# A hybrid decoder block on one core: low halves of the projection weights kept in DRAM after the first token group, and pick indices laid out in pairs

## The chip, the cores and the metric

One core of one Trainium2 chip runs the whole block for one sequence of 1024 tokens. The metric is the device time of one execution in microseconds (us), the median of several executions. Engines are named as the profile names them: PE (TensorE matmul), PEld (its weight loads), DVE (VectorE), ACT (ScalarE), POOL (GpSimd) and SP (SyncE, which here only issues DMAs).

## What is computed

The reference is a decoder block in fp32 with width 1024. Cut to what matters here:

```python
h = rms_norm(x, norm1_g) * (1 + sc1) + sh1          # adaLN: mod = silu(c) @ w_ada + b_ada
b, c, hc, q, k, v = split(h @ w_in)                 # 2304 columns
mixed = concat(short_conv(b, c, hc), window_attention(q, k, v))
x = x + g1 * (mixed @ w_out)                        # 1024 columns
h2 = rms_norm(x, norm2_g) * (1 + sc2) + sh2
# PEER: 8 heads, two key tables of 128, top 16 of each, top 16 of the 256 sums
q = h2 @ wq                                         # 2048 columns
sa, sb = q_a @ keys_a, q_b @ keys_b
eidx, top = top16(top16(sa) + top16(sb))            # an expert = one row of u and of v
x = x + g2 * sum_k softmax(top)_k * gelu(u[eidx_k] . h2) * v[eidx_k]
```

## The kernel before, in words

**Two phases.** The front computes everything up to the choice of the experts, for three groups of tokens in turn (`GROUPS`: 384, 384 and 256 tokens). The dense phase then runs PEER for the first 640 tokens as two large matrix products over all 16384 experts (L816 with the table `uT`, L873 with `v`), while a background task gathers the chosen rows for the last 384 tokens (L741, L760, L768).

**Precision.** Each fp32 factor is split into a high part, rounded to fp32r, and the low rest; a product is high times high, high times low and low times high. For a weight, ACT rounds it (`wH`, L268) and POOL subtracts (`wL`, L269).

**Projections.** `proj` (L260 to L274) makes 128 output columns of `w_in`, `w_out` or `wq` for one group. It goes in two half chunks of 512 rows: SP fetches 256 KB of weights (`wraw`, L265), ACT makes `wH`, POOL makes `wL`, and PE runs 12 matmuls (L272). Each of the three tiles has three buffers. A group calls it 18 + 8 + 16 = 42 times, so each group has 84 half chunks and the front has 252. Every group fetches and splits the same weights again.

**Order of the work.** The front is written in program order and a scheduler lays out each engine's queue; on the chip every queue runs in order. `bg` lets background tasks advance. Into the first group these are the adaLN products (`ada`) and the bias table. Into the second and third group it is the previous group's `finish_topk`, which runs `select` and then `spread` or `place` for each block of 128 tokens.

**`select`** (L593 to L671) runs per block. It copies the indices of the key picks to bf16 (`idf`, L595), forms 64 candidate sums per head (`cand`, L598), takes the top 16 of them (`top16`), decodes their positions, and picks the two indices by one-hot tiles (`hot1`): compare with `rank` (L660), multiply by the indices (L662), add up in halves (L666, L668). The index operand of L662 has the stride 0 in its innermost dimension.

**`spread`** (five blocks in all) turns each token's picks into one-hot tiles `oi` (in the pattern ACT, POOL, DVE, DVE over the tokens, L703 to L706) and `oj` (DVE, L711), multiplies them on PE (L714), copies the result to `stage` (ACT, L715) and writes `stage` to DRAM (`gd`, SP, L717).

**SP's queue** holds the weight fetches (L265), the `x` chunks (L306), the row stores (L519), the stores of `h2` (L533), the `stage` stores (L717), the adaLN fetches (L157) and at the end of the front the first loads of the dense phase (L796, L827, L937).

Of the kernel before, what the change touches and what calls it, by code (L numbers as in the profile page):

```python
# [10 lines left out]
F32 = mybir.dt.float32  # L11
F32R = mybir.dt.float32r
BF16 = mybir.dt.bfloat16
# [3 lines left out]
ALU = mybir.AluOpType  # L17
# [4 lines left out]
P = 128  # L22
# [4 lines left out]
PH = 8  # L27
# [15 lines left out]
NCAND = CSTART[-1]  # L43
# [31 lines left out]
def hymba_peer_kernel(ctx: ExitStack, tc: tile.TileContext, a, out: bass.AP):  # L75
    nc = tc.nc
    V, A, G, PE = nc.vector, nc.scalar, nc.gpsimd, nc.tensor

    const = ctx.enter_context(tc.tile_pool(name="const", bufs=1))
    dram = ctx.enter_context(tc.tile_pool(name="dram", bufs=1, space=DRAM))  # L80
# [23 lines left out]
    def col(name, i=0):  # L104
        return cols[:, COLS[name][0] + i:COLS[name][0] + i + 1]
# [7 lines left out]
    h2s = dram.tile([2, P, NC, DT], F32, name="h2s")  # L113
    gd = dram.tile([DT // TB, P, P, TB], F32, name="gd")
    biasd = dram.tile([P, NH, 384], F32, name="biasd")

    cond = const.tile([P, 8], F32, name="cond")
    A.activation(cond, colr("c"), AF.Silu)
# [8 lines left out]
    wp = fe.enter_context(tc.tile_pool(name="wp", bufs=3))  # L127
    hot = ExitStack()
    lv = hot.enter_context(tc.tile_pool(name="lv", bufs=1, side="right"))
    sel = hot.enter_context(tc.tile_pool(name="sel", bufs=1, side="right"))  # L130
# [96 lines left out]
    def bg(us):  # L227
        for t in list(tasks):
            t[2] += us * t[1]
            while t[2] >= 1.0:  # L230
                t[2] -= 1.0
                with tc.high_priority(offset=-BACK):
                    end = next(t[0], 0) == 0
                if end:
                    tasks.remove(t)
                    break
# [12 lines left out]
    def bigt(pool, name, dt, cnt=2):  # L249
        return [pool.tile([P, 4, TM], dt, name=f"{name}{i}", tag="big") for i in range(cnt)]  # L250

    def tmp(name, w=TM, **k):
        if name == "q":
            k["bufs"] = QB
        return tp.tile([P, w], F32, name=name, **k)

    def ch(t, c):
        return t[c // 4][:, c % 4, :]

    def proj(wsrc, sH, sL, T):  # L260
        bg(24 * T / 2400 + 0.5)
        pt = pj.tile([P, TM], F32, name="pj")
        for h in range(2):
            w = wp.tile([P, 4, P], F32, name="wraw")
            nc.sync.dma_start(w, wsrc[:, 4 * h:4 * h + 4, :])  # L265
            wH = wp.tile([P, 4, P], F32R, name="wH")
            wL = wp.tile([P, 4, P], F32R, name="wL")
            A.copy(wH, w)  # L268
            G.tensor_tensor(wL, w, wH.bitcast(F32), op=ALU.subtract)  # L269
            for c in range(4):  # L270
                for k, (wl, sr) in enumerate(((wH, sH), (wH, sL), (wL, sH))):
                    PE.matmul(pt[:, 0:T], wl[:, c, :], sr[h][:, c, 0:T],  # L272
                              start=(h == 0 and c == 0 and k == 0), stop=(h == 1 and c == 3 and k == 2))
        return pt[:, 0:T]  # L274
# [29 lines left out]
    def xchunk(c, t0, T):  # L304
        x = tmp("x", bufs=XB)[:, 0:T]
        nc.sync.dma_start(x, a["xT"][:, c, t0:t0 + T])  # L306
        return x
# [24 lines left out]
    def front(t0, T, hs, nxt):  # L332
        nb = T // P
        nd = max(0, min(nb, (DT - t0) // P))
        hH, hL = hs
        kH = t1.tile([P, P + TM], F32R, name="kH")
        kL = t1.tile([P, P + TM], F32R, name="kL")
        if t0:
            A.copy(kH[:, 0:P], kpH.bitcast(F32))
            A.copy(kL[:, 0:P], kpL.bitcast(F32))  # L340
        kc = tmp("k", bufs=1)[:, 0:T]
        A.copy(kc, proj(a["w_in"][4], hH, hL, T))
        qT = [tmp("y", bufs=4)[:, 0:T] for c in range(4)]
        for c in range(4):
            A.copy(qT[c], proj(a["w_in"][c], hH, hL, T))
        vT = tmp("q")
        A.copy(vT[:, 0:T], proj(a["w_in"][5], hH, hL, T))

        def conv():
            ys = []  # L350
            for cc in range(4):
                cs = tmp("q")[:, 0:T]
                A.copy(cs, proj(a["w_in"][6 + 3 * cc], hH, hL, T))
                yield
                u = tp.tile([P, TM + 2], F32, name="u", bufs=1)
                V.tensor_copy(u[:, 0:2], upv[:, cc, :])
                V.tensor_tensor(u[:, 2:T + 2], cs, proj(a["w_in"][7 + 3 * cc], hH, hL, T), op=ALU.mult)
                yield
                V.tensor_copy(upv[:, cc, :], u[:, T:T + 2])
                y = tmp("y", bufs=4)[:, 0:T]  # L360
                A.activation(y, u[:, 0:T], AF.Copy, scale=col("cw", cc))
                V.scalar_tensor_tensor(y, u[:, 1:T + 1], col("cw", 4 + cc), y, op0=ALU.mult, op1=ALU.add)
                V.scalar_tensor_tensor(y, u[:, 2:T + 2], col("cw", 8 + cc), y, op0=ALU.mult, op1=ALU.add)
                V.tensor_tensor(y, y, proj(a["w_in"][8 + 3 * cc], hH, hL, T), op=ALU.mult)
                ys.append(y)
                yield
            bc = group_stats(ys, T)
            if CY:
                yield
            for cc, y in enumerate(ys):  # L370
                V.scalar_tensor_tensor(y, y, col("cg", cc), bc(cc), op0=ALU.mult, op1=ALU.mult)
                A.copy(mc[0][:, cc, 0:T], y)
                G.tensor_tensor(mc[1][:, cc, 0:T], y, mc[0][:, cc, 0:T].bitcast(F32), op=ALU.subtract)
# [110 lines left out]
        mH, mL = (mc[0], ma[0]), (mc[1], ma[1])  # L484
# [3 lines left out]
            rn = norm_stats(lambda c: xchunk(c, *nxt), nxt[1]) if nxt else None  # L488
        x2T = bigt(ba, "x2T", F32)
        for c in range(NC):  # L490
            pt = proj(a["w_out"][c], mH, mL, T)
            V.scalar_tensor_tensor(ch(x2T, c)[:, 0:T], pt, mod[:, 16 + c:17 + c], xchunk(c, t0, T),
                                   op0=ALU.mult, op1=ALU.add)
        h2 = bigt(bb, "h2H", F32R), bigt(bb, "h2L", F32R)
        h2H, h2L = h2
# [45 lines left out]
        iu = [lv.tile([P, 2 * PH, 16], U32, name="iu", bufs=5) for b in range(nb)]  # L541
# [14 lines left out]
        for mm in range(0, 16, 2):  # L556
            qs = []
            for m in (mm, mm + 1):
                qq = tmp("q")[:, 0:T]
                A.copy(qq, proj(a["wq"][m], h2H, h2L, T))  # L560
                qs.append(qq)
                if held and m % 2 == KLAG:
                    keys(*held)
                    held = None
            held = (mm, mm + 1), qs
# [25 lines left out]
            V.max_index(u[:, 8:16], v[:, 8:16], s)  # L591

    def select(va, iu):  # L593
        idf = sel.tile([P, 2 * PH, 16], BF16, name="idf")
        A.copy(idf, iu)  # L595
        va4 = va.rearrange("p (h s) k -> p h s k", s=2)
        id4 = idf.rearrange("p (h s) k -> p h s k", s=2)
        cand = sel.tile([P, PH, NCAND], F32, name="cand")  # L598

        def pairs(a0, na, nbb, st):  # L600
            o4 = cand[:, :, st:st + na * nbb].rearrange("p h (x y) -> p h x y", y=nbb)
# [24 lines left out]
        def ft(name, **k):  # L626
            return sel.tile([P, n], F32, name=name, **k)
# [29 lines left out]
        for s, src in ((0, aab), (1, stb)):  # L657
            r = ft(f"pick{s}", tag=("a3", "st3")[s])
            hot1 = sel.tile([P, PH, 16, 16], BF16, name="hot1")
            V.tensor_tensor(hot1, src.rearrange("p (h k) -> p h k", h=PH).unsqueeze(2).to_broadcast([P, PH, 16, 16]),  # L660
                            rank.unsqueeze(1).to_broadcast([P, PH, 16, 16]), op=ALU.is_equal)
            V.tensor_tensor(hot1, hot1, id4[:, :, s, :].unsqueeze(3).to_broadcast([P, PH, 16, 16]), op=ALU.mult)  # L662
            yield
            m = 8
            while m > 1:
                V.tensor_tensor(hot1[:, :, 0:m, :], hot1[:, :, 0:m, :], hot1[:, :, m:2 * m, :], op=ALU.add)  # L666
                m //= 2
            V.tensor_tensor(r.rearrange("p (h k) -> p h k", h=PH), hot1[:, :, 0, :], hot1[:, :, 1, :], op=ALU.add)  # L668
            yield
            res.append(r)  # L670
# [349 lines left out]
    with tc.tile_pool(name="ada", bufs=2, side="right") as ap:  # L1020
        T0 = GROUPS[0][1]
        wt = gat.tile([P, 4, D], F32, name="wt", tag="stage")
        slots = [wt[:, c, :] for c in range(4)]
        x0 = bigt(bb, "x0", F32)
        wide = [t.rearrange("p c t -> p (c t)")[:, 0:D] for t in bigt(ba, "wringa", F32) + bigt(bb, "wringb", F32)]
        first = ada_start(ap, slots[0:3] + wide, slots[3])
        next(first)
        for h in range(2):
            nc.sync.dma_start(x0[h][:, :, 0:T0], a["xT"][:, 4 * h:4 * h + 4, 0:T0])

        def x0c(c):
            return ch(x0, c)[:, 0:T0]

        for _ in range(3):
            next(first)
        r0 = norm_stats(x0c, T0)
        for c in range(NC):
            G.tensor_tensor(x0c(c), x0c(c), r0[:, 0:T0], op=ALU.mult)
        for _ in first:
            pass  # L1040
        hs = norm1(*GROUPS[0], x0c)
        table.append(add(bias_table(ap), 1.0))
        rest.append(add(ada((2, 4, 3, 5), ap, slots), ADA_RATE, ADA0))
        hs, prev = front(*GROUPS[0], hs, nxts[0])
        for t in rest:
            drain(t)
    gbc = tc.tile_pool(name="gb", bufs=1, side="right")
# [82 lines left out]
```

## Time and profile before

| | us |
|---|---|
| median of three executions | 2853.47 |
| lowest and highest | 2850.66 and 2859.0 |
| the profiled execution, its own time | 2857.49 |
| its span in the profile | 2855.7 |

The span is 1.8 us shorter than the profiled execution's own time. Busy times are sums over an engine's instructions; PE and PEld overlap each other, and a PE busy time counts pipelined matmuls to their modelled ends. A wait row names who waited, for whom, for how long in sum, how often, and the longest.

### The profile page before, as it was taken

The page shows a single profiled execution, that of the slowest core. Times are in us where ns is not written, and L with a number is a line of the kernel's source. Part 1 is how long each engine was busy: PE and PEld are TensorE (multiplying, and loading weights), DVE is VectorE, ACT ScalarE, POOL GpSimd, SP SyncE. Part 2 cuts the span into 40 slices and gives each one's busy share as a digit, 9 for nine tenths or more (in the row PEclk, how much of TensorE's full clock was granted, in tenths as well). Part 3 has the DMA queues.
Part 4 walks back from the last instruction along what each step waited for, and adds up shares of the span by engine and source line. Part 5 has one row for each costly group of instructions (what it writes and reads, how often), then busy time and mean ns, then how long its engine had stood idle before and what let it go on. Part 6 is the DMA issues. An engine that isn't in the chain of part 4 may idle for free.

```text
span 2855.7 us, 45148 instructions
## 1 busy us (share of the span) xinstructions
PE 2700.5 (95%) x15679; PEld 2445.9 (86%) x15679; DVE 2373.4 (83%) x4845; ACT 1093.9 (38%) x2193; POOL 1721.7 (60%) x1491
## 2 busy tenths in 40 slices
PE   8899988999787889999999999999999999999998
PEld 6788978789786778889989989999989889988987
DVE  3665898877899697888988888888889888888887
ACT  2455468775586643222322222232222222222221
POOL 3444475656667744666666666666666666666661
PEclk7999999999999989999999999999999999999999
DMA  7647423464344677999999999999999999999995
GB/s 243 217 155 232 121 103 115 158 216 156 97 151 137 234 227 229 342 337 343 326 322 346 340 344 335 349 325 332 347 334 324 325 339 346 333 336 345 324 327 193
DMA packets 345157, 764.31 MB, mean 268 GB/s; under 512 B 31296, under 2 KB 130016, under 8 KB 341984
## 3 DMA queue, kind: packets, MB, share of 16 engines
q0 software_dynamic: 112320, 408.99, 39.6%
q1 hardware_dynamic: 231168, 349.81, 37.4%
q8 instruction: 123, 2.02, 0.3%
q10 hardware_dynamic: 1440, 2.62, 0.2%
q14 instruction: 106, 0.87, 0.1%
HBM read 702.06 MB, written 59.24 MB: 267 GB/s over the span
## 4 chain that ended last, share of the span: by engine, by line
PE 44%; DMA 8%; DVE 6%; issue 5%; POOL 2%; ACT 1%; SPq 0%; DVEq 0%; POOLq 0%; ACTq 0%
PE pv L873 22%; PE pa L816 21%; DMA vraw<-in_v 4%; DMA uraw<-in_uT 2%; DVE pq L768 2%; DVE vdL L860 1%; POOL rows L741 1%; ACT vdH L859 1%; DVE rows L760 1%; DMA wraw<-in_wq 1%; DMA rows<-in_v,eidx 1%; POOL uL L800 1%; DVE dacc L892 0%; DVE gw L835 0%; PE pj L272 0%
## 5 line engine op out<-in xcount | busy, mean ns | idle before, releaser
L816 PE MATMUL pa<-h,uH 128*128 128x320 f32 x4096 | 772.9, 311 | 15.2 <-ACT uH L799 6.2
L816 PEld LDWEIGHTS pa<-h,uH 128*128 128x128 f32 x4096 | 648.8, 189 | 23.1 <-ACT uH L799 7.2
L873 PE MATMUL pv<-vdH,wdH 128*128 128x512 f32 x1275 | 500.0, 392 | 18.0 <-DVE dacc L892 16.4
L269 POOL TENSOR_TENSOR wL<-wraw,wH 128x512 fp32r<-128x512 f32 x252 | 351.5, 1402 | 272.7 <-ACT wH L268 249.4
L873 PE MATMUL pv<-vdL,wdH 128*128 128x512 f32 x1275 | 497.8, 390 | 0.1
L873 PE MATMUL pv<-vdH,wdL 128*128 128x512 f32 x1275 | 496.8, 390 | 0.0
L816 PE MATMUL pa<-h,uL 128*128 128x320 f32 x2048 | 469.2, 310 | 2.3 <-POOL uL L800 2.3
L800 POOL TENSOR_TENSOR uL<-uraw,uH 128x512 fp32r<-128x512 f32 x256 | 342.4, 1338 | 163.3 <-ACT uH L799 142.7
L741 POOL DMA_INDIRECT rows<-in_u,eidx x257 | 260.8, 1015 | 157.1 <-DVE aw L760 83.2
L741 POOL DMA_INDIRECT rows<-in_v,eidx x254 | 253.7, 999 | 164.6 <-DVE pq L768 117.1
L816 PEld LDWEIGHTS pa<-h,uL 128*128 128x128 f32 x2048 | 344.6, 189 | 3.3 <-POOL uL L800 3.3
L768 DVE SCALAR_TENSOR_TENSOR pq<-rows,aw,pq 128x1024 f32<-128x1024 f32 x253 | 324.5, 1282 | 3.3 <-DMA rows<-in_v,eidx 0.8
L892 DVE TENSOR_TENSOR dacc<-dacc,pv 128x512 f32<-128x512 f32 x310 | 211.9, 684 | 134.0 <-PE pv L873 111.4
L859 ACT CAST vdH<-vraw 128x512 fp32r<-128x512 f32 x255 | 153.5, 619 | 439.0 <-DMA vraw<-in_v 366.4
L799 ACT CAST uH<-uraw 128x512 fp32r<-128x512 f32 x256 | 158.3, 619 | 418.9 <-DMA uraw<-in_uT 340.5
L760 DVE CUSTOM_DVE_ANT_0 rows<-rows,pq 128x1024 f32<-128x1024 f32 x257 | 307.5, 1212 | 12.5 <-DMA rows<-in_u,eidx 10.9
L873 PEld LDWEIGHTS pv<-vdH,wdH 128*128 128x128 f32 x1275 | 239.6, 188 | 74.9 <-DVE dacc L892 24.7
L873 PEld LDWEIGHTS pv<-vdH,wdL 128*128 128x128 f32 x1275 | 239.8, 188 | 50.9
L873 PEld LDWEIGHTS pv<-vdL,wdH 128*128 128x128 f32 x1275 | 239.8, 188 | 47.3 <-DVE vdL L860 0.5
L706 POOL TENSOR_SCALAR oi<-iota,tr 128x128 f32<-128x128 f32 x160 | 198.5, 1243 | 96.2 <-PE gps L714 88.1
L860 DVE TENSOR_TENSOR vdL<-vraw,vdH 128x512 fp32r<-128x512 f32 x255 | 192.1, 770 | 71.7 <-ACT vdH L859 66.7
L842 ACT CAST wdH<-gw 128x640 fp32r<-128x640 f32 x128 | 93.0, 728 | 377.0 <-DVE gw L835 342.4
(257 smaller groups left out, 5085.7 us busy)
## 6 DMA issues: line engine op xcount, KB each, us to landing
uraw<-in_uT SPq DMA_DIRECT2D x256, 256.0 KB
vraw<-in_v SPq DMA_DIRECT2D x255, 256.0 KB
gd<-stage SPq DMA_DIRECT2D x20, 2048.0 KB
gt<-gd SPq DMA_DIRECT2D x160, 256.0 KB
wraw<-in_w_in SPq DMA_DIRECT2D x108, 256.0 KB
wraw<-in_wq SPq DMA_DIRECT2D x96, 256.0 KB
wt<-in_w_ada SPq DMA_DIRECT2D x40, 512.0 KB
wraw<-in_w_out SPq DMA_DIRECT2D x48, 256.0 KB
```

The lines of the kernel that those rows point to most:

```text
L269: G.tensor_tensor(wL, w, wH.bitcast(F32), op=ALU.subtract)
L706: (G if who == "P" else V).tensor_scalar(oi, iota, tr[:, 0, t:t + 1], tr[:, 2, t:t + 1], op0=ALU.is_equal, op1=ALU.mult)
L741: G.indirect_dma_start(out=r, out_offset=None, in_=table, in_offset=bass.IndirectOffsetOnAxis(ap=eidx[:, ti, k:k + 1], axis=0))
L760: V.tensor_tensor_reduce(out=r, in0=r, in1=h2, op0=ALU.mult, op1=ALU.add, scale=1.0, scalar=0.0, accum_out=aw[:, k:k + 1])
L768: V.scalar_tensor_tensor(acc, r, aw[:, k:k + 1], acc, op0=ALU.mult, op1=ALU.add)
L799: A.copy(uH, raw)
L800: G.tensor_tensor(uL, raw, uH.bitcast(F32), op=ALU.subtract)
L816: PE.matmul(AT[j][:, s, 0:n], l[:, c, :], h2[r][4 * h + c][:, s * n:s * n + n], start=(h == 0 and c == 0 and k == 0), stop=(h == 1 and c = ...
L859: A.copy(vH, raw)
L860: V.tensor_tensor(vL, raw, vH.bitcast(F32), op=ALU.subtract)
L873: PE.matmul(pt, l[:, P * tt:P * tt + P], r, start=(m == 0), stop=(m == 3 * J - 1))
L892: V.tensor_tensor(dst, dst, pt, op=ALU.add)
```

## The change

In the first group each low part that POOL has made is also stored to a DRAM tile of its own, from SP's queue, after POOL has made the next-but-one. In the second and third group `wL` is fetched from there by SP; POOL does not subtract. `wL` has four buffers where it had three. `idf` holds each index twice, so that L662's index operand ends in a contiguous pair; ACT fills it by two copies. `cand` and `hot1` share one slot.

```diff
@@ proj
-    def proj(wsrc, sH, sL, T):
+    def save(keep):
+
+        while len(unsaved) > keep:
+            key, wL = unsaved.pop(0)
+            lows[key] = dram.tile([P, 4, P], F32, name="low_{}{}{}".format(*key))
+            nc.sync.dma_start(lows[key], wL.bitcast(F32))
+
+    def proj(name, m, sH, sL, T):
+        wsrc = a[name][m]
...
-            wL = wp.tile([P, 4, P], F32R, name="wL")
+            wL = wp.tile([P, 4, P], F32R, name="wL", bufs=4)
             A.copy(wH, w)
-            G.tensor_tensor(wL, w, wH.bitcast(F32), op=ALU.subtract)
+            if (name, m, h) in lows:
+                nc.sync.dma_start(wL.bitcast(F32), lows[name, m, h])
+            else:
+                G.tensor_tensor(wL, w, wH.bitcast(F32), op=ALU.subtract)
+                save(1)
+                unsaved.append(((name, m, h), wL))
@@ select
-        idf = sel.tile([P, 2 * PH, 16], BF16, name="idf")
-        A.copy(idf, iu)
+        idf = sel.tile([P, 2, PH * 16, 2], BF16, name="idf")
+        iu4 = iu.rearrange("p (h s) a -> p h s a", s=2)
+        for s in range(2):
+            A.copy(idf[:, s].rearrange("p (h a) y -> p h a y", h=PH),
+                   iu4[:, :, s, :].unsqueeze(3).to_broadcast([P, PH, 16, 2]))
...
-        cand = sel.tile([P, PH, NCAND], F32, name="cand")
+        cand = sel.tile([P, PH, NCAND], F32, name="cand", tag="hot1")
...
-            V.tensor_tensor(hot1, hot1, id4[:, :, s, :].unsqueeze(3).to_broadcast([P, PH, 16, 16]), op=ALU.mult)
+            hk = hot1.rearrange("p h a (k y) -> p (h a) k y", y=2)
+            V.tensor_tensor(hk, hk, idf[:, s].unsqueeze(2).to_broadcast([P, PH * 16, 8, 2]), op=ALU.mult)
@@ after the first group's front
+        save(0)
```

## Rows read from the trace of the kernel before

**Rows 1.** The page's part 1: busy us, share of the span, instructions

```profile
PE 2700.5 (95%) x15679; PEld 2445.9 (86%) x15679; DVE 2373.4 (83%) x4845; ACT 1093.9 (38%) x2193; POOL 1721.7 (60%) x1491
```

**Rows 2.** Windows: stretch and length, busy us by engine, PEclk, DMA share, GB/s

```profile
52.00:352.00 300.00, 281.60 (x1553) 252.74 (x1553) 196.06 (x645) 140.29 (x306) 139.61 (x102) 0.95 0.59 187
352.00:725.00 373.00, 337.87 (x2130) 305.78 (x2129) 314.92 (x1037) 253.36 (x600) 234.00 (x184) 0.98 0.42 146
725.00:1025.00 300.00, 249.27 (x1850) 226.48 (x1848) 253.71 (x902) 195.28 (x463) 210.61 (x161) 0.97 0.47 159
350.00:550.00 200.00, 171.93 (x1092) 150.78 (x1091) 188.12 (x574) 143.38 (x355) 126.41 (x98) 0.97 0.32 114
800.00:950.00 150.00, 122.12 (x914) 110.61 (x912) 138.27 (x368) 111.12 (x272) 109.13 (x84) 0.98 0.44 155
1057.00:2850.00 1793.00, 1768.60 (x9887) 1606.66 (x9888) 1554.17 (x2065) 481.64 (x785) 1111.68 (x1022) 1.00 0.93 325
```

**Rows 3.** The chain that ended last, in order of time: start, us, what

```profile
999.08 5.86 PE pj L272 x48
...
1009.88 2.91 DMA wraw<-in_wq
```

**Rows 4.** Waits of PEld, 352 to 725 us: us in total, times, longest

```profile
PEld pj L272 <- POOL wL L269: 5.3, 3, 3.1
```

**Rows 5.** Waits of PEld, 725 to 1025 us

```profile
PEld pj L272 <- POOL wL L269: 15.9, 13, 5.9
```

**Rows 6.** Groups of POOL instructions, 352 to 1025 us

```profile
L269 POOL TENSOR_TENSOR wL<-wraw,wH 128x512 fp32r<-128x512 f32 x160 | 224.4, 1409 | 120.5 <-ACT wH L268 114.0 <-DVE gsum L620 1.8 <-PE pj L272 1.8
L706 POOL TENSOR_SCALAR oi<-iota,tr 128x128 f32<-128x128 f32 x160 | 198.5, 1243 | 96.2 <-PE gps L714 88.1 <-ACT tr L690 5.7 <-DVE oi L706 0.8
```

**Rows 7.** Groups of DVE instructions by shape, 352 to 1025 us

```profile
L706 DVE TENSOR_SCALAR oi<-iota,tr 128x128 f32<-128x128 f32 x320 | 123.5, 424 | 22.9 <-PE gps L714 21.5
L711 DVE TENSOR_TENSOR oj<-iota,tr 128x512 f32<-128x512 f32 x160 | 122.4, 783 | 4.7 <-PE gps L714 2.8 <-ACT tr L690 1.4 <-issue 0.2
```

**Rows 8.** Single lines, whole span: min/median/max ns, first and last start

```profile
L706 DVE TENSOR_SCALAR oi<-iota,tr x320: 240/340/1379, 378.5 to 968.8; 128x128 f32<-128x128 f32 x160
L711 DVE TENSOR_TENSOR oj<-iota,tr x160: 637/683/1793, 377.3 to 967.0; 128x512 f32<-128x512 f32 x160
L660 DVE TENSOR_TENSOR hot<-stb,rank x8: 1200/1210/2317, 369.4 to 1088.2; 128x2048 bf16<-128x2048 bf16 x8
L662 DVE TENSOR_TENSOR hot<-hot,idf x16: 2265/2283/3369, 362.8 to 1091.6; 128x2048 bf16<-128x2048 bf16 x16
```

**Rows 9.** DVE in order of time: start, us, instruction

```profile
355.55 0.75 DVE L602 TENSOR_TENSOR cand<-va 128x128 f32<-128x128 f32 x3
...
361.50 1.37 DVE L650 TENSOR_TENSOR st<-st,st 128x128 f32<-128x128 f32 x1
...
367.95 0.28 DVE L652 TENSOR_TENSOR st<-st,st 128x128 f32<-128x128 f32 x1
```

**Rows 10.** POOL in order of time, 357 to 370 us

```profile
357.76 4.95 POOL L269 TENSOR_TENSOR wL<-wraw,wH 128x512 fp32r<-128x512 f32 x3 [7.90 <-ACT wH L268]
```

**Rows 11.** Waits of SP's own queue, 352 to 725 us

```profile
SPq L265 <- POOL wL L269: 218.0, 70, 16.1
SPq L717 <- ACT stage L715: 44.7, 6, 19.3
SPq L717 <- ACT oi L703: 17.5, 4, 14.7
```

**Rows 12.** Waits of SP's own queue, 725 to 1025 us

```profile
SPq L717 <- ACT oi L703: 18.5, 2, 12.5
...
SPq L717 <- ACT stage L715: 15.2, 3, 13.9
```

**Rows 13.** Windows in which DMA is fuller, columns as in the second group

```profile
50.00:100.00 50.00, 45.24 (x206) 37.02 (x206) 23.74 (x26) 13.80 (x26) 20.93 (x16) 0.90 0.76 248
1040.00:1050.00 10.00, 6.58 (x34) 6.06 (x33) 9.97 (x29) 0.75 (x4) 0.95 (x1) 0.84 1.10 354
```

More of the change, by code (lines that the diff above doesn't have):

```diff
@@ L115, in hymba_peer_kernel @@
     biasd = dram.tile([P, NH, 384], F32, name="biasd")
+    lows, unsaved = {}, []
     cond = const.tile([P, 8], F32, name="cond")
@@ L341, in front @@
         kc = tmp("k", bufs=1)[:, 0:T]
-        A.copy(kc, proj(a["w_in"][4], hH, hL, T))
+        A.copy(kc, proj("w_in", 4, hH, hL, T))
         qT = [tmp("y", bufs=4)[:, 0:T] for c in range(4)]
         for c in range(4):
-            A.copy(qT[c], proj(a["w_in"][c], hH, hL, T))
+            A.copy(qT[c], proj("w_in", c, hH, hL, T))
         vT = tmp("q")
-        A.copy(vT[:, 0:T], proj(a["w_in"][5], hH, hL, T))
+        A.copy(vT[:, 0:T], proj("w_in", 5, hH, hL, T))
         def conv():
@@ L352, in conv @@
                 cs = tmp("q")[:, 0:T]
-                A.copy(cs, proj(a["w_in"][6 + 3 * cc], hH, hL, T))
+                A.copy(cs, proj("w_in", 6 + 3 * cc, hH, hL, T))
                 yield
@@ L356, in conv @@
                 V.tensor_copy(u[:, 0:2], upv[:, cc, :])
-                V.tensor_tensor(u[:, 2:T + 2], cs, proj(a["w_in"][7 + 3 * cc], hH, hL, T), op=ALU.mult)
+                V.tensor_tensor(u[:, 2:T + 2], cs, proj("w_in", 7 + 3 * cc, hH, hL, T), op=ALU.mult)
                 yield
@@ L363, in conv @@
                 V.scalar_tensor_tensor(y, u[:, 2:T + 2], col("cw", 8 + cc), y, op0=ALU.mult, op1=ALU.add)
-                V.tensor_tensor(y, y, proj(a["w_in"][8 + 3 * cc], hH, hL, T), op=ALU.mult)
+                V.tensor_tensor(y, y, proj("w_in", 8 + 3 * cc, hH, hL, T), op=ALU.mult)
                 ys.append(y)
@@ L490, in front @@
         for c in range(NC):
-            pt = proj(a["w_out"][c], mH, mL, T)
+            pt = proj("w_out", c, mH, mL, T)
             V.scalar_tensor_tensor(ch(x2T, c)[:, 0:T], pt, mod[:, 16 + c:17 + c], xchunk(c, t0, T),
@@ L559, in front @@
                 qq = tmp("q")[:, 0:T]
-                A.copy(qq, proj(a["wq"][m], h2H, h2L, T))
+                A.copy(qq, proj("wq", m, h2H, h2L, T))
                 qs.append(qq)
@@ L593, in select @@
     def select(va, iu):
-        idf = sel.tile([P, 2 * PH, 16], BF16, name="idf")
-        A.copy(idf, iu)
+        idf = sel.tile([P, 2, PH * 16, 2], BF16, name="idf")
[3 more added lines that the diff above has]
+                   iu4[:, :, s, :].unsqueeze(3).to_broadcast([P, PH, 16, 2]))
         va4 = va.rearrange("p (h s) k -> p h s k", s=2)
-        id4 = idf.rearrange("p (h s) k -> p h s k", s=2)
-        cand = sel.tile([P, PH, NCAND], F32, name="cand")
+        cand = sel.tile([P, PH, NCAND], F32, name="cand", tag="hot1")
         def pairs(a0, na, nbb, st):
```

## The prediction
> **What bounds the kernel now.** I read the shares of busy time first [rows 1]: PE 95%, DVE 83%, POOL 60%. Those are averages over two phases, so the windows come next [rows 2]. From 1057 to 2850 us PE is busy 1768.6 of 1793 us at full clock, and nothing in that phase is edited. It is a block of fixed length, so the end moves by as much as the front ends earlier or later. The front ends near 1025 us and has three stretches: 52 to 352 us (first group), 352 to 725 (second) and 725 to 1025 (third). Second and third last 673 us. There DVE is busy 314.9 + 253.7 = 568.6 us, PE 587.1, POOL 444.6. Inside them lie two stretches where DVE is nearly full: 188.1 of 200 us (350 to 550) and 138.3 of 150 (800 to 950). These are the stretches of `select` and `spread`; there PE's queue waits for one-hot tiles from DVE, ACT and POOL. So the front after the first group is bound by DVE in about half its length, and by a chain of hand-overs elsewhere.
>
> POOL's work there is two groups of almost the same size [rows 6]: 160 subtractions `wL` with 224.4 us (the other 8 of the 168 that the code makes for these groups lie before 352 us), and 160 one-hot tiles with 198.5 us. PE's waits for `wL` are small: 5.3 us in the second group [rows 4], 15.9 us in the third [rows 5].
>
> POOL also costs DVE time. Two DVE instructions of one shape lie 6 us apart [rows 9]: L650 took 1.37 us, L652 0.28 us. During the first one POOL ran three subtractions back to back for 4.95 us [rows 10]. The one-hot tiles of DVE show it in bulk: L706 takes 424 ns in the mean, L711 783 ns [rows 7], against minima of 240 and 637 ns [rows 8].
>
> **The change part by part.**
>
> *Subtractions removed.* 168 of 252 go. The direct gain is PE's wait for them, 5.3 + 15.9 = 21.2 us [rows 4, 5]. The next in line for the same matmuls is the fetch of `wL` or ACT's `wH`, so not all of it goes: bounds 0 and 21 us. I take 14, nearer the upper end, because a fetch is issued three half chunks ahead, see below.
>
> *DVE freed from POOL.* Against its minima L706 loses 320 x (424 - 240) = 58.9 us and L711 160 x (783 - 637) = 23.4 us, together 82.3 us [rows 7, 8]. Of POOL's busy time 224.4 of 444.6 us, or 50%, goes [rows 2, 6]. So DVE gets back about 41 us. Lower bound 0 (the remaining `oi` of POOL run at the same time as DVE's and may hold it as much as before), upper bound 82.
>
> *Pairs.* L662 takes 2283 ns with stride 0 innermost; L660, of the same size and type, with a contiguous innermost run, 1210 ns [rows 8]. If a run of two is enough, each of 16 gains 1.07 us. Twelve lie in the two groups, 12.9 us; four lie at the start of the dense phase. Bounds: 0 and 1.07 each; I take L660's value, the nearest row of that size.
>
> *From DVE time to end time.* 41 + 12.9 = 54 us. Of DVE's 568.6 us, 326.4 us or 57% lie in the two full stretches [rows 2]: 31 us. PE is itself busy 172 of 200 and 122 of 150 us there, so I count 70%: 22 us. Bounds 0 and 54. The four late multiplications, 4.3 us, I count half: 2 us.
>
> *POOL's one-hot tiles* no longer stand behind subtractions that wait for ACT (114 us of idle time before `wL` in these groups [rows 6]). The nearest row for PE's wait on POOL is that for its other line, 21.2 us, so the bounds are 0 and 21. I take 2, because a token's tiles also need DVE's and ACT's share, which come late more often.
>
> *Fetches added.* 168 x 256 KB = 44 MB in 673 us, where DMA is 42% and 47% busy [rows 2]. At the 354 GB/s that a full window shows [rows 13], they take 124 us of the some 375 us of free DMA time. One wait for a weight fetch on the chain lasted 2.91 us [rows 3]. PE needs 5.86 us for 48 matmuls with 256 columns [rows 3], so 1.47 us per half chunk: with four buffers three half chunks, 4.4 us, cover the fetch, and more in the second group, where matmuls have 384 columns. But every fetch also stands in SP's queue and waits for the buffer of four half chunks before. SP already waits 218 us in the second group, for `wL` [rows 11]; that wait turns into one for PE and ACT. Behind it stand `x`, row stores, `stage` stores and the dense phase's first loads. Bounds 0 and 50 us (priced in the last rival), taken 2.
>
> *Stores added.* 84 stores, 22 MB, in the first group, where DMA is 59% busy [rows 2]: 62 us of 123 us free. The fullest window, 50 to 100 us, has 76% [rows 13]; 84 stores in 300 us are 14 in 50 us, 3.7 MB, which need 10 of its 12 free us. Behind each store on SP stands the next `wraw`, which waited for the same subtraction anyway. Bounds 0 and 12 (that window's free time), taken 3: the adaLN fetches share it.
>
> *`cand` in `hot1`'s slot.* Before, the next block's candidate sums start while the last block is still decoding: L602 at 355.55 us fills such a gap, the picks follow [rows 9]. Afterwards they wait for the last pick. All of it is DVE's own work in order, so the cost is only ACT hand-overs left bare, 0 to 10 us, taken 2. The second copy for `idf` is ACT's, busy 253.4 of 373 us in the second group [rows 2]: nothing, and at most a hold of ACT before the picks, inside the same bound. The fourth `wL` buffer costs no time.
>
> *Sum.* 14 + 22 + 2 + 2 - 2 - 3 - 2 = 33 us. The profiled execution took 2857.5 us (span 2855.7), so 2824.5; the median of the runs is 4.0 us lower: 2820.5, rounded to 2820.
>
> **The rivals.** A measurement of this kernel can tell 0.3%, 8.6 us, from no change.
>
> *More than I count.* The freed DVE time passes on in full, 54 us, PE's waits go, 21 us, with 4 us from the late multiplications: 79 us, 2774. For it: DVE's full stretches. Against it: PE is busy 587 of 673 us there, so 86 us is all that PE could give. A rule makes this case larger than the minima do. The Trainium skill, "SBUF — State Buffer", on the shared port pair, says that GpSimd and VectorE take it as an exclusive lock for a whole instruction and the later one is fully blocked. The 1.37 us row agrees. By that rule alone each of the 160 subtractions could block DVE for up to its own length, and the sum would go by PE's limit of 86 us, an estimate that gives 2767. The rule also leaves POOL's `oi` to block DVE as before, which is why I keep the half.
>
> *No change.* The half chunks are paced by ACT's `wH` and by PE's in-order queue as much as by POOL, and the fetch takes over the waits: 0 to 8 us, 2849. For it: PE waits for `wL` only 21 us of 673. That the pair doesn't double L662's rate is part of this: 12.9 x 0.57 x 0.7 = 5 us less than forecast, no more.
>
> *Slower: SP's queue.* Before, `wraw` and `wL` together let SP run up to six half chunks ahead; now a fetch can't pass the fourth. When SP holds for a `stage` store, PE is fed only for 4 x 1.47 = 5.9 us, less 2.9 us for the landing, so 3 us. SP held for L717 44.7 + 17.5 us in the second group and 18.5 + 15.2 us in the third, 95.9 us in 15 holds [rows 11, 12]. If each falls on PE beyond 3 us, that is 51 us, and with the other gains of 35 us (33 without the 2 for fetches) the kernel takes 16 us longer: 2869. It decides once PE's wait for the fetch is above 35 us. Against it: half chunks come at 373 / 84 = 4.4 us each in the second group, so four last 17.8 us, and only the longest holds, of 19.3 us, reach past that.
>
> **How the numbers follow.** Forecast, 9 to 60 us less: 0.66. More: 0.14. No change: 0.10. Slower: 0.10. So faster 0.80, same 0.10, slower 0.10. The range leaves out 0.1 on the slow side, and on the fast side the extreme of the larger case: 2772 to 2851.
>
> **What would show it.** Right: 84 `wL` subtractions by POOL; the mean of L706 on DVE near 340 ns and of L711 near 700; L662 near 1.2 us; first matmul of the dense phase near 1025 us with the phase's length unchanged; little PE wait on the fetch. Wrong: L706 still above 400 ns (POOL's `oi` hold DVE as before); PE waits for `wL`'s fetch above 20 us; the first group longer than its 300 us by more than 10 us; or a dense phase that grows by what the front loses, since its DMA is 93% busy [rows 2].

## The result and the profile after

The changed kernel takes 2821.5 us in the median of four executions (2812.6 to 2827.8), the kernel before 2856.2 us beside it. The ratio is 0.9877 with a 95% interval of 0.984 to 0.9915. Timed again beside other kernels it came to 2821.2 us and 0.9873 (0.9852 to 0.9893). The forecast was 2820 us.

The page's part 1 of the kernel after, from an execution of 2812.6 us with a span of 2810.5, answers to [rows 1]:

```profile
PE 2686.1 (96%) x15679; PEld 2443.0 (87%) x15679; DVE 2291.3 (82%) x4845; ACT 1090.2 (39%) x2201; POOL 1493.4 (53%) x1323
```

POOL lost 228 us of work and DVE 82 us. The end moved by 45 us in this execution and by 35 in the medians.

To see where it moved, take two marks that all kernels here have: ACT's copy of the key projection `k`, the first thing a group's front produces, and ACT's last copy of a PEER query `q`, the last projection of the front. The rows give count, min/median/max ns, and the first and last start. The first fence is the kernel before, the second the kernel after; its L356 and L574 are L342 and L560 before.

```profile
L342 ACT COPY k<-pj x3: 367/475/478, 59.2 to 729.2; 128x384 f32<-128x384 f32 x2, 128x256 f32<-128x256 f32 x1
...
L560 ACT COPY q<-pj x48: 354/471/485, 265.3 to 1022.1; 128x384 f32<-128x384 f32 x32, 128x256 f32<-128x256 f32 x16
```

```profile
L356 ACT COPY k<-pj x3: 365/470/478, 60.4 to 710.3; 128x384 f32<-128x384 f32 x2, 128x256 f32<-128x256 f32 x1
...
L574 ACT COPY q<-pj x48: 354/472/482, 266.5 to 973.7; 128x384 f32<-128x384 f32 x32, 128x256 f32<-128x256 f32 x16
```

With the middle copy (342.7 us before, 348.1 after) they give the length of each stretch; "rest" runs from the last query to the end of the span. The second execution of the kernel after shows how far a stretch varies from one execution to the next.

| us | first group | second | third | rest |
|---|---|---|---|---|
| before | 283.5 | 386.5 | 292.9 | 1833.6 |
| after | 287.7 | 362.2 | 263.4 | 1836.8 |
| after, second execution | 289.6 | 363.1 | 262.2 | 1847.5 |

The front is 48 us shorter in both. The first group pays 4 to 6 us, the second gains 23 to 24 and the third 30. The rest, which the prediction took as fixed, is 3 to 14 us longer. Two executions do not settle that size: over the profiles of all kernels here, whose code for the rest hardly differs, it lies between 1830.5 and 1847.5 us.

**DVE.** The groups that answer to [rows 7], for the second and third group of the kernel after:

```profile
L728 DVE TENSOR_TENSOR oj<-iota,tr 128x512 f32<-128x512 f32 x160 | 108.2, 692 | 4.9 <-PE gps L731 3.0 <-ACT tr L707 0.3
L723 DVE TENSOR_SCALAR oi<-iota,tr 128x128 f32<-128x128 f32 x320 | 103.4, 360 | 38.6 <-PE gps L731 36.5 <-ACT h2H L315 0.4
```

The narrow tiles (`oi`, 128x128) went from 424 to 360 ns in the mean, the wide ones (`oj`, 128x512) from 783 to 692: 34 us less busy time for the same work. (A group's busy time counts overlapping instructions once, so it is less than count times mean.)

What POOL was running at the same time tells why. Sorted by that, the tiles of the kernel before took (mean ns, number of tiles in brackets; the other 9 and 6 ran beside other subtractions of POOL):

| | beside no POOL instruction | beside POOL's tiles alone | beside a `wL` subtraction |
|---|---|---|---|
| narrow | 338 (55) | 353 (210) | 819 (46) |
| wide | 670 (4) | 686 (119) | 1101 (31) |

Against the medians of [rows 8], 340 and 683 ns, the last column is 35 us too long in sum, and 34 us went. One narrow tile of the kernel before and the subtraction beside it, then, in the second fence, one wide tile of the kernel after and the two POOL tiles beside it (start, us, instruction):

```profile
445.48 1.31 DVE L706 TENSOR_SCALAR oi<-iota,tr 128x128 f32<-128x128 f32 x1
445.34 1.37 POOL L269 TENSOR_TENSOR wL<-wraw,wH 128x512 fp32r<-128x512 f32 x1
```

```profile
444.87 0.68 DVE L728 TENSOR_TENSOR oj<-iota,tr 128x512 f32<-128x512 f32 x1
444.82 2.51 POOL L723 TENSOR_SCALAR oi<-iota,tr 128x128 f32<-128x128 f32 x2 [7.45 <-PE gps L731]
```

The line of the multiplication by the indices, over the whole span of the kernel after, answers to the last of [rows 8]:

```profile
L679 DVE TENSOR_TENSOR hot<-hot,idf x16: 1175/1222/1232, 362.2 to 1051.1; 128x2048 bf16<-128x2048 bf16 x16
```

A contiguous run of two elements is enough here: a median of 2283 ns became 1222.

**PE's waits.** Waits of PEld from 340 to 1020 us, the kernel before in the first fence, the kernel after in the second:

```profile
PEld pj L272 <- POOL wL L269: 21.2, 16, 5.9
PEld gps L714 <- DVE oi L706: 18.9, 20, 3.5
...
PEld gps L714 <- ACT stage L715: 9.4, 13, 2.1
PEld pj L272 <- ACT wH L268: 9.0, 5, 4.5
PEld gps L714 <- POOL oi L706: 6.7, 14, 1.2
```

```profile
PEld gps L731 <- ACT stage L732: 15.8, 17, 5.7
PEld pj L286 <- ACT wH L277: 11.4, 11, 3.5
...
PEld pj L286 <- DMA wL<-low_wq: 3.4, 4, 1.5
...
PEld gps L731 <- POOL oi L723: 2.3, 5, 1.0
PEld pj L286 <- DMA wL<-low_w_in: 2.0, 1, 2.0
...
PEld gps L731 <- DVE oi L723: 1.5, 3, 1.0
```

The wait for POOL's `wL` became 5.4 us for its fetch. The wait for DVE's one-hot tiles, which the prediction named without a price of its own, almost vanished (18.9 to 1.5 us). Next in line are ACT's stage copies and `wH`.

PE is now close to full in these groups. The windows of the kernel after answer to the second and third of [rows 2], with the same columns:

```profile
348.00:710.00 362.00, 341.27 (x2220) 314.74 (x2220) 289.04 (x1120) 258.55 (x617) 135.48 (x105) 0.99 0.63 217
710.00:974.00 264.00, 238.24 (x1815) 222.57 (x1813) 211.06 (x861) 191.74 (x457) 93.68 (x79) 0.96 0.73 254
```

PE is busy 579.5 of 626 us, where it was 587.1 of 673. Its idle time fell from 86 to 46 us.

**What the rest gave back.** The chain in order of time behind the last projection, for the kernel after and, in the second fence, before (start, us, what):

```profile
983.52 6.41 DMA h<-h2s
989.94 6.67 DMA gt<-gd
996.68 13.90 DMA uraw<-in_uT
```

```profile
1032.08 6.59 DMA h<-h2s
1038.68 6.64 DMA gt<-gd
1045.70 8.09 DMA uraw<-in_uT
```

The third load takes 6 us longer at the same place of the chain; in the second execution of the kernel after it took 14.4 us. What lengthens it was not tried, and the remainder of the difference is not explained.

### The profile page after: what moved, and what is told of

The parts are those of the page before. It is cut to its first block, busy times and chain, and to the rows that moved or that the text cites. A ratio compares the mean times of both kernels' runs of the same rounds, so it can differ in the third digit from the quotient of the medians.

```text
span 2810.5 us, 45275 instructions
## 1 busy us (share of the span) xinstructions
PE 2686.1 (96%) x15679; PEld 2443.0 (87%) x15679; DVE 2291.3 (82%) x4845; ACT 1090.2 (39%) x2201; POOL 1493.4 (53%) x1323
## 4 chain that ended last, share of the span: by engine, by line
PE 53%; DVE 8%; DMA 7%; issue 3%; ACT 2%; POOL 0%; SPq 0%; DVEq 0%; ACTq 0%; POOLq 0%
PE pv L890 26%; PE pa L833 24%; DMA vraw<-in_v 3%; PE pj L286 2%; PE gps L731 1%; DMA wraw<-in_wq 1%; DVE pq L785 1%; DVE vdL L877 1%; DVE rows L777 1%; DMA rows<-in_u,eidx 1%; DVE gw L852 1%; DVE wdL L860 0%; DMA uraw<-in_uT 0%; DVE dacc L909 0%; ACT vdH L876 0%
## 5 line engine op out<-in xcount | busy, mean ns | idle before, releaser
L723 POOL TENSOR_SCALAR oi<-iota,tr 128x128 f32<-128x128 f32 x160 | 204.5, 1281 | 348.6 <-PE gps L731 158.0
L277 ACT CAST wH<-wraw 128x512 fp32r<-128x512 f32 x252 | 154.3, 618 | 169.5 <-PE pj L286 85.3
```

The source lines that it names most:

```text
L723: (G if who == "P" else V).tensor_scalar(oi, iota, tr[:, 0, t:t + 1], tr[:, 2, t:t + 1], op0=ALU.is_equal, op1=ALU.mult)
```

## The experiments

Each ran beside the kernel before. Ratios are to the kernel before, with 95% intervals.

### The two parts, each alone

The first kernel has the pairs and `cand` in `hot1`'s slot, and no stored low parts. The second has the stored low parts and the shared slot (which makes room for the fourth buffer), with the old `idf` and multiply. The third has the shared slot alone.

```diff
 pairs_only
-            wL = wp.tile([P, 4, P], F32R, name="wL", bufs=4)
+            wL = wp.tile([P, 4, P], F32R, name="wL")
...
-                save(1)
-                unsaved.append(((name, m, h), wL))
 lows_oldmul (and `idf` as before)
-            V.tensor_tensor(hk, hk, idf[:, s].unsqueeze(2).to_broadcast([P, PH * 16, 8, 2]), op=ALU.mult)
+            V.tensor_tensor(hot1, hot1, id4[:, :, s, :].unsqueeze(3).to_broadcast([P, PH, 16, 16]), op=ALU.mult)
 slot_only (against the kernel before)
-        cand = sel.tile([P, PH, NCAND], F32, name="cand")
+        cand = sel.tile([P, PH, NCAND], F32, name="cand", tag="hot1")
```

> The pairs alone (with cand in hot1's slot); all groups subtract on POOL. Theory M (the prediction's: DVE time freed from POOL's holds is the largest gain, PE's waits for the low part come next, the pairs are worth 12.9 us of DVE time x 0.57 x 0.7 + 2 = 7 us): 2856 - 7 = 2849 us, ratio 0.9975; L662's successor near 1.2 us. Theory W (what paid is that PE's and ACT's chain no longer runs through POOL): 2853 to 2856 us. Theory P (the pairs pay most, because DVE is full where they run): 2836 us or less.

> The stored low parts alone (four buffers, cand in hot1's slot), the multiply with the old stride 0. Theory M: 2856 - 35 + 7 = 2828 us, ratio 0.990. Theory W: 2822 us, as the whole change. Theory P: 2840 us or more.

> The whole change once more, timed beside the others, to set it against the stored low parts with the old multiply (ratio 0.9852). Theory N (the pairs add nothing once the low parts are fetched, because both free the same DVE): ratio between 0.983 and 0.988, overlapping. Theory G (the pairs cost time there): 0.988 or more. The prediction's sum (pairs worth 7 us) asked for 0.983 or less.

> The kernel before with one edit: cand in hot1's slot; old multiply, nothing stored or fetched. Theory C (the shared slot only takes fillers from DVE, as the prediction's 0 to 10 us): 2857 to 2861 us, ratio 1.000 to 1.002, so that the pairs alone were worth 12 us or more. Rival O (the gain of the kernel with pairs alone came from the new order that the slot forces on select): 2850 us or less, ratio 0.997 or less.

| | median us | ratio |
|---|---|---|
| pairs and slot | 2846.2 | 0.9958 (0.9942 to 0.9973) |
| slot alone | 2868.1 | 1.004 (1.0026 to 1.0054) |
| low parts and slot, old multiply | 2813.5 | 0.9852 (0.9834 to 0.987) |
| whole change, again | 2821.2 | 0.9873 (0.9852 to 0.9893) |

The shared slot alone costs 0.4%, 11 us (7 to 15 by the interval): both theories about it fell, and the forecast's 0 to 10 us holds at its upper end at best. Why it costs that much was not tried. So the pairs alone are worth 1.004 - 0.9958 = 0.8%, some 23 us, against 7 in the sum. With the slot's cost in it the first kernel came to 2846.2 us, between theory M's 2849 and theory P's 2836; the second, at 2813.5, was faster than any of the three theories had it. But once the low parts are fetched, the pairs add nothing that can be measured: the intervals of 0.9852 and 0.9873 overlap, and the fronts end at 975.6 us without the pairs and 973.7 with them. The two parts do not add up: 0.9958 x 0.9852 / 1.004, with the slot counted once, would be 0.977. Theory N's ratio came true; that both draw on the same DVE time is its reading, and the next experiments bear on it. The low parts with neither pairs nor shared slot were not run.

### Does POOL's work cost DVE, or only PE?

Here the low part is fetched into three buffers, and POOL runs an instruction whose result nobody reads, once for each half chunk of the second and third group: first a subtraction with two tensor inputs, then a multiplication with one. (The extra tile takes the room of the fourth buffer, so the comparison is the three-buffer kernel, which follows below.)

```diff
                 nc.sync.dma_start(wL.bitcast(F32), lows[name, m, h])
+                junk = wp.tile([P, 4, P], F32R, name="junk", bufs=1)
+                G.tensor_tensor(junk, wH.bitcast(F32), wH.bitcast(F32), op=ALU.subtract)   # dummy_b3
+                G.tensor_scalar(junk, wH.bitcast(F32), 1.0, None, op0=ALU.mult)            # dummy1_b3, instead
```

> As the three-buffer kernel, and in the second and third group POOL also subtracts into a tile that nobody reads (168 instructions back on POOL, off PE's path). Theory M: the holds on DVE return, 41 us of DVE time x 0.57 x 0.7 = 16 us more than the three-buffer kernel; the mean of the one-hot tiles on DVE back near 424 ns. Theory W: within 5 us of the three-buffer kernel.

> As the kernel with the unread subtraction on POOL (2873 us), but POOL's extra instruction multiplies one tile by a constant: one tensor input where the subtraction had two. Theory L2 (DVE is held by POOL's two-input instructions; POOL's one-input tiles cost it nothing, since giving them to DVE left the means at 350 and 694 ns): tiles on DVE stay near 360 and 697 ns and the total near the three-buffer kernel's 2840 us, at most 2850. Theory Q (what costs is POOL's queue: its own one-hot tiles stand behind the extra instructions, and wH's buffers are held longer): 2860 us or more with the tiles on DVE near 360 ns.

The subtraction nobody reads: 2873.2 us, ratio 1.0046 (1.0028 to 1.0065), 33 us over the three-buffer kernel's 2839.7. The multiplication: 2862.8 us, 1.0026 (1.001 to 1.0043), 23 us over it. DVE groups from 340 to 1020 us, of the three-buffer kernel, of the kernel with the subtraction, and of the one with the multiplication:

```profile
L728 DVE TENSOR_TENSOR oj<-iota,tr 128x512 f32<-128x512 f32 x160 | 108.5, 697 | 6.1 <-ACT tr L707 2.6 <-PE gps L731 2.2
L723 DVE TENSOR_SCALAR oi<-iota,tr 128x128 f32<-128x128 f32 x320 | 103.1, 358 | 44.6 <-PE gps L731 42.1
```

```profile
L725 DVE TENSOR_SCALAR oi<-iota,tr 128x128 f32<-128x128 f32 x320 | 121.4, 417 | 38.8 <-PE gps L733 37.2
L730 DVE TENSOR_TENSOR oj<-iota,tr 128x512 f32<-128x512 f32 x160 | 115.3, 737 | 4.9 <-ACT tr L709 2.6 <-PE gps L733 1.0
```

```profile
L725 DVE TENSOR_SCALAR oi<-iota,tr 128x128 f32<-128x128 f32 x320 | 114.5, 396 | 51.8 <-PE gps L733 47.7 <-issue 2.2
L730 DVE TENSOR_TENSOR oj<-iota,tr 128x512 f32<-128x512 f32 x160 | 111.1, 710 | 5.7 <-ACT tr L709 2.6 <-PE gps L733 1.1
```

With the subtraction the narrow tiles are back at 417 ns of the 424 of before, though their own code is untouched and PE does not read what POOL makes. So POOL's subtractions lengthen DVE's instructions; theory W, for which nothing should have changed, fell. Of the narrow tiles, the 52 that ran beside an unread subtraction took 703 ns, those beside POOL's tiles alone 352; of the wide ones, 25 took 921 against 692. The two kinds of tiles together have 25 us more busy time. That the total grew by 33 us, where the forecast was 16, suggests that more than DVE's time is involved.

The multiplication shows what else. It lengthens DVE's tiles by about half as much, though each takes 1.6 us (168 of them 268.9 us), so theory L2 fell. Its total was in theory Q's range, the tiles' mean of 396 ns was not. Waits of PEld in that kernel, 340 to 1020 us:

```profile
PEld gps L733 <- POOL oi L725: 22.0, 30, 1.9
```

In the three-buffer kernel that wait is 2.7 us: POOL's own one-hot tiles stand behind the extra work in its queue. Both kernels also hold `wH` longer: ACT waits 16 to 17 us for POOL there, where it waited 7.2 us for the subtraction in the kernel before. So POOL's work costs time in up to three ways (DVE held, POOL's own tiles late, `wH` held), and these runs do not divide the 23 to 33 us among them.

### POOL's and ACT's share of the one-hot tiles

`HOT` names, for four tokens in turn, the engine that makes the narrow tile: A for ACT, P for POOL, V for DVE.

```diff
-HOT = "APVV"
+HOT = "AVVV"    # hot_avvv
+HOT = "VPVV"    # hot_vpvv
```

> The whole change with POOL's quarter of the one-hot tiles given to DVE (320 become 480 on DVE), so that POOL does next to nothing in the second and third group. Theory L (a POOL instruction holds DVE back while it runs): the tiles on DVE fall to a mean near 250 ns and the wide ones near 645 ns, DVE's sum for both goes from 211.6 to about 223 us, total 2815 to 2828 us. Theory W (POOL only mattered through its place in the chain): means stay near 345 and 690 ns, DVE gets 55 us more to do, 2835 us or more.

> The whole change with ACT's quarter of the one-hot tiles given to DVE (ACT makes each by two instructions of some 400 ns, DVE by one of 350). Theory A (after the change PE waits for ACT: 15.8 us for the stage copies and 11 for ACT's tiles, and DVE has room): 2800 to 2815 us. Rival V (DVE is still the bound of those stretches): 2822 us or more.

With no tiles on POOL: 2818.4 us, ratio 0.9866 (0.9845 to 0.9887), as the whole change. DVE groups, 340 to 1020 us:

```profile
L723 DVE TENSOR_SCALAR oi<-iota,tr 128x128 f32<-128x128 f32 x480 | 145.8, 350 | 24.7 <-PE gps L731 22.3 <-ACT h2H L315 0.4 <-ACT tr L707 0.2
L728 DVE TENSOR_TENSOR oj<-iota,tr 128x512 f32<-128x512 f32 x160 | 108.7, 694 | 2.5 <-PE gps L731 1.8 <-ACT tr L707 0.3
```

The means hardly move (360 to 350, 692 to 694) when POOL's 160 tiles of 1.28 us go. So these held DVE by at most 10 ns a tile. That DVE has 480 narrow tiles here and not 320 does not hide a hold: the run below has 480 as well and POOL's tiles in place, with means of 359 and 691 ns. The 463 narrow and 150 wide tiles that overlap no POOL instruction took 341 and 686 ns, which is what the tiles take without POOL; theory L's 250 and 645, close to the minima of [rows 8], are not. Theory L's range for the time held, but not for its reason. Theory W's means came true, its time did not: DVE took 43 us more work (254.5 against 211.6) and the kernel was not slower. PE's wait for these tiles is 3.4 us: DVE was no longer what the stretch waited for.

With no tiles on ACT: 2826.4 us, 0.9888 (0.9866 to 0.9911). No gain, so theory A fell: PE's wait for ACT's stage copies rose from 15.8 to 23.2 us although ACT had less to do. Rival V's time came true, but PE's waits for DVE's tiles in that kernel are 3.9 us, so DVE is not shown to be the bound. With PE busy 93% of the second and third group of the changed kernel, little is left to win from moving tiles between the other engines. That also fits the pairs, which free DVE alone and add nothing once the low parts are fetched.

### The depth of the fetch

```diff
 bufs3
-            wL = wp.tile([P, 4, P], F32R, name="wL", bufs=4)
+            wL = wp.tile([P, 4, P], F32R, name="wL")
 wraw2_wl5
-            w = wp.tile([P, 4, P], F32, name="wraw")
+            w = wp.tile([P, 4, P], F32, name="wraw", bufs=2)
...
-            wL = wp.tile([P, 4, P], F32R, name="wL", bufs=4)
+            wL = wp.tile([P, 4, P], F32R, name="wL", bufs=5)
 buf4_only (nothing is stored, so nothing is fetched)
-                save(1)
-                unsaved.append(((name, m, h), wL))
```

> The whole change with three buffers for the low part instead of four. Theory M: the fourth buffer is cover that is rarely used, 2821 to 2826 us. Rival S (the look-ahead of SP's queue is what decides): PE waits for the fetch above 20 us and 2836 us or more.

> The whole change with five buffers for the low part and two for the raw weights (the same room). Theory S (the depth of the fetch of the low part binds, as three buffers cost 18 us): PE's wait for the fetch falls below 3 us and the total to 2812 us or less. Rival T (past four the raw weights' own depth binds): PE and ACT wait for the raw weights, 2830 us or more.

> Pairs and the fourth buffer for the low part, all groups subtract on POOL, no stores, no fetches. Theory F (the fourth buffer pays because a fetch must be issued that far ahead; POOL's own product needs no such lead): 2846 us as pairs alone, within 4. Rival B (one more buffer helps any producer): 2836 us or less.

Three buffers: 2839.7 us, 0.9936 (0.9918 to 0.9953), 18 us slower than the whole change. Rival S's time came true; PE's wait for the fetch, which it put above 20 us, came to 18.5 us with 0.4 us for `w_out`. Waits of PEld, 340 to 1020 us, in the three-buffer kernel:

```profile
PEld pj L286 <- DMA wL<-low_wq: 9.5, 8, 2.8
PEld pj L286 <- DMA wL<-low_w_in: 8.6, 4, 2.9
```

With a fourth buffer the two are 3.4 and 2.0 us. Before the fetch, the fourth buffer was worth nothing: pairs with four buffers took 2844.1 us, 0.9954 (0.9936 to 0.9972), as pairs with three. So theory F holds. A fifth, paid for with a raw-weight buffer, made it 2853.8 us, 0.9982 (0.9969 to 0.9995). PE's wait for the fetch then all but goes (0.9 us), but its waits for ACT's `wH` rise to 20.0 us, and the first group takes 313.8 us instead of 287.7. ACT waits 111 us for raw weights in that group, 42 us in the changed kernel: rival T.

### What the stores cost

```diff
-            if (name, m, h) in lows:
-                nc.sync.dma_start(wL.bitcast(F32), lows[name, m, h])
-            else:
-                G.tensor_tensor(wL, w, wH.bitcast(F32), op=ALU.subtract)
+            G.tensor_tensor(wL, w, wH.bitcast(F32), op=ALU.subtract)
+            if (name, m, h) not in lows:
```

> Pairs, four buffers and the first group's 84 stores, but all groups subtract on POOL and nothing is fetched back. Theory M (stores almost hidden): the first group, k copy to k copy, some 288 us against 281.8 with pairs alone, total 2846 + 5 = 2851 us. Rival D (stores crowd DMA or hold SP): 2860 us or more, and later groups unchanged.

2853.8 us, ratio 0.9991 (0.9977 to 1.0006). The kernel with pairs and four buffers but no stores has 0.9954, so the stores cost 0.37%, some 10 us. The first group takes 289.8 us against 281.5, close to theory M's 288; rival D's 2860 us fell. The waits of DVE in it, without stores (first fence) and with them:

```profile
DVE acc L162 <- DMA wt<-in_w_ada: 6.5, 6, 2.4
```

```profile
DVE acc L162 <- DMA wt<-in_w_ada: 19.1, 8, 6.6
```

So DVE waits longer for the adaLN fetches, as the prediction said, and by more. That DMA is shared does not explain it: these fetches took a median of 4.8 us from issue to landing without the stores and 5.0 us with them. The longest wait, 6.6 us, was for one that landed in 4.5 us; it was issued late, right behind a store that SP had held for 2.7 us until POOL was done:

```profile
218.69 0.33 SPq L266 DMA_DIRECT2D low_w_out<-wL  x1
219.07 0.78 SPq L158 DMA_DIRECT2D wt<-in_w_ada  x1
```

How much of the 10 us the queue costs and how much the fuller DMA was not tried. The raw weights did land later, those of `w_in` after a median of 4.2 us instead of 3.2.

## Why the prediction was right, and which of its terms were not

The time fell at 2821.5 us against 2820, and the mechanism, POOL freed and DVE and PE with it, is what the runs show. The terms of the sum were not all right; several errors cancelled, and that the two times lie so close is luck.

- **DVE freed from POOL: 41 us forecast, 34 us measured on the same two lines.** The number came out of two wrong steps. The minima of [rows 8] are not the undisturbed durations; the medians there, 340 and 683 ns, are, so the excess was not 82 us but 320 x 84 + 160 x 100 ns = 43 us. And POOL's tiles have next to no share in it, so not half of it goes but the 35 us of the subtractions.
- **From DVE time to end time: 57% x 70%.** The front gained 48 us where the sum, without the late multiplications, has 31. The other terms do not make up the difference, so this step was too small; no run measures it alone.
- **PE's wait for the low part: 14 us of 21.2 forecast.** 5.4 us of wait for the fetch came in its place, so 16 went; the wait for `wH` rose by 2.
- **POOL's one-hot tiles: 2 us of 0 to 21.** The prediction priced this by POOL's other line, though PE's wait for these tiles has a row of its own: 6.7 us before, 2.3 after.
- **Pairs: 7 us with the late ones.** Each gained 1.06 us as forecast. What it is worth at the end was wrong: some 23 us in the kernel before, nothing measurable in the changed one. The 57% x 70% was a constant for something that depends on what else waits for DVE.
- **The shared slot: 2 us of 0 to 10.** In the kernel before, alone, it costs 11 (7 to 15).
- **Stores: 3 us of 0 to 12.** 10 us by themselves.
- **Look-ahead of the fetch: cover of three half chunks.** Right for four buffers, with 5.4 us of wait. The price was close by: one buffer less costs 18 us. The rival on SP's queue asked for more than 35 us of that wait and did not come true.
- **The dense phase as a fixed block.** The rest is 3 to 14 us longer, which took back part of the front's 48 us. The sign "first matmul of the dense phase near 1025 us" was misplaced: that matmul starts at 1025.4 us in the kernel before and at 976.8 us after.

The front's gain was larger than its part of the sum (48 us against 31), and the rest took the surplus back. The Trainium skill, "SBUF — State Buffer", on the shared port pair, would have a VectorE instruction with two SBUF inputs blocked by any GpSimd instruction that reads SBUF and started first. The subtractions fit it: `oj`, which has two such inputs, took 1101 ns beside them. POOL's 160 tiles, which read `iota` from SBUF, do not: 100 of the 160 `oj` of the changed kernel began while one of them was running and took 687 ns, and the run that moves them away has a mean of 694 against 692. The larger rival that leaned on that rule, 2767 us, did not come true.

No run here is shown to beat the changed kernel. The one without the pairs is lower in the median (2813.5), inside the intervals.

## What to carry to other kernels

A subtraction that is repeated for every group can be cheaper to fetch than to make, even from an engine that PE hardly waits for, if that engine slows a fuller one. Look for its price in the fuller engine's durations: sort them by what the other engine was running at the same time, and take the undisturbed ones as the baseline, not the minimum. A fetch in the place of an engine's product needs its buffers counted anew: here the fourth was worth nothing to the product and 18 us to the fetch. Two edits that free the same engine need not add up, and a tile slot that two tensors share can have a price of its own.

## What the runs showed of the hardware

- POOL's instructions did not all touch DVE alike. 168 subtractions of 128x512 with two tensor inputs (1.17 us each) lengthened DVE's narrow tiles by 59 ns in the mean. 168 multiplications with one input, although they ran 1.6 us each, did by 38 ns. 160 one-hot tiles of 128x128 (1.28 us each) did by 10 ns at most.
- The hold falls on the instructions that overlap: a narrow DVE tile beside a `wL` subtraction took 819 ns in the mean, beside POOL's one-hot tiles 353, beside nothing on POOL 338.
- A bf16 multiplication of 128x2048 whose second operand repeats runs of two elements took 1222 ns; with single repeated elements 2283 ns.
- Stores of 22 MB in the first 290 us, where DMA was 59% busy in the mean, raised the landing time of the `w_in` weights from 3.2 to 4.2 us (medians); that of the adaLN weights went only from 4.8 to 5.0 us.
